# A streaming encoder layer on one core: other ticks for the heads' values, another start, a fixed order, and another order of the first convolution products

## The chip, the cores and the metric

The kernel runs on one core of one Trainium2 chip. Its time is the device time of one execution in microseconds (us). Three executions of the kernel before gave a median of 2348.04 us, the lowest 2346.84 and the highest 2348.41. One further execution was taken with the profiler; it took 2346.67 us, and its profile and trace are the ones read here. The engines are named as the profile names them: PE is the matrix engine, PEld its loads of the stationary operand, DVE the vector engine, ACT the scalar engine, POOL the third elementwise engine, and SP the engine whose queue issues most transfers (DMAs).

## What is computed

One layer of a hybrid encoder for 512 prompt frames and 64 frames of a running stream, 2048 channels wide, all in float32. Cut to what matters:

```python
hn = rmsnorm(x, g_norm1)
q, k, v, gb, gc, hc = split(hn @ w_in)            # 8 heads of 128, then 3 x 1024 for the convolution
q, k = rmsnorm(q, g_q), rmsnorm(k, g_k)           # per head
z = q @ k.T / sqrt(128)                           # strictly causal, 128-query blocks, cached keys first
log_1mb = where(mask, log_sigmoid(-z), 0)
after = reverse_cumsum(log_1mb) - log_1mb
o_attn = where(mask, exp(log_sigmoid(z) + after), 0) @ v      # stick-breaking weights
u = gc * hc
o_conv = gb * (conv_w[0]*u[t-2] + conv_w[1]*u[t-1] + conv_w[2]*u[t])
x = x + concat(rmsnorm(o_attn), rmsnorm(o_conv)) @ w_out
h2 = rmsnorm(x, g_norm2)
x = x + (silu(h2 @ w_gate) * (h2 @ w_up)) @ w_down
```

It returns the new frames, the new keys and values and the state of the convolution.

## The kernel before

**Numbers and tiles.** The 512 + 64 frames lie as 576 columns, cut into two halves of 288. A float32 product is made of three: each operand is split into a rounded high part and a remainder (`hi`/`lo`, `whi`/`wlo`, `ph`/`pl`, `vh`/`vl`), and high by high, low by high and high by low are added up in one accumulator. The high part is a cast, mostly on ACT (`cast`, line 727); the low part is a subtraction on DVE (`low`, line 730), which reads the cast. So each operand of PE costs one ACT and one DVE instruction, in this order.

**Stages.** In the order of time: *frames* (to about 33 us): x is loaded, turned by PE (`turn_samples`, line 384, for the 64 stream frames of a group of channels; `turn_x`, line 390, for the 512 others), copied by ACT into a tile `st` (lines 397, 399), and split by DVE into the two parts of `x` (lines 406, 407), while PE already multiplies by the first weight. *Projections* (to about 161 us): first whole products with `whi`/`wlo`, then, from about 72 us on, products that are cut into seven by sums of quarters (`unit_prepare` and `unit_run`; a product p_ of unit n is written (n, p_)). The sums of frames that these need are made by `x_sums` (lines 662 to 697, with DVE instructions on lines 677, 678, 680 and 681), one pair of channel groups after another. *Heads* (about 161 to 404 us): PE does the remaining projections (`pj`, line 246), and between their matmuls the work of the attention heads. *Convolution* (up to about 800 us, its own seven products per unit, `conv_prepare` and `conv_run`), mixed with the first parts of what follows; then the output projection and the feed-forward part.

**What sets the order.** Each engine runs its own queue in program order and waits at the head of it. The heads are generators: `attend(h)` yields at ticks. A tick is one step of a projection on PE, three matmuls of 288 columns. Head h starts PERIOD = 49 ticks after head h-1, so at any time the later ticks of one head lie between the early ticks of the next: tick 79 of a head and tick 30 of the next are the same moment. What a head does at its tick t is queued when PE's program has come to that tick. `until(t)` (line 745) waits for tick t.

In one head, `E` are the turned queries and keys, `sums` their squares' sums on DVE (line 777), `ss` the product that adds them up (line 784), `z` the scores, `ph`/`pl` the two parts of the log-weights `pb` of a query block, `zb` the sums over keys (lines 887 to 906), `limit` the step from these sums to the weights (DVE line 880, ACT line 882, cast), `vtok` the values, loaded back by `load_values`, `po` the product of weights and values (lines 931 and 934), `sp` and `cz` (lines 946 to 949) the sums for the 64 stream frames ("the sample"), and `os` their output.

Parts of the program run under a *manual schedule*: there the named engines keep the order in which the program is written; elsewhere the compiler's own scheduler may move instructions of an engine past each other. Before, the frames stage has a manual schedule for ACT, DVE and SP, the projections up to the units one for SP alone, and the units and heads one for ACT, DVE and POOL as well (`unit_mode`, line 1162).

In the convolution `corder` lists the products in PE's order, and `begin` says after which of them the next is prepared. `conv_prepare` makes the operand by sums on DVE (lines 1341 to 1359), a cast on ACT (1352) and a subtraction on DVE (1355). A column of raw weights is free, and the next one is loaded on SP (line 1318), when the last product that needs it has been prepared. `load_sum(q)` loads one of the three stored sums of frames, `xs_t`, of 2304 KB.

Of the kernel before, what the change touches and what calls it, by code (L numbers as in the profile page):

```python
# [98 lines left out]
def tile_hybrid_stream_step(  # L99
# [287 lines left out]
    def turn_x(kt, c, k, sc, pss):  # L387
        psx = ps_z.tile([P, 512], F32, tag=f"z{kt % 3}", name=f"psx{kt}")
        for i in range(4):
            nc.tensor.transpose(psx[:, i * P : (i + 1) * P], xin[c][:, i, k * P : (k + 1) * P], ident)  # L390
        if kt < NH:
# [11 lines left out]
        if kt >= 9 and kt % 2:  # L403
# [20 lines left out]
    with tc.manual_schedule(engines={mybir.EngineType.Activation, mybir.EngineType.DVE, mybir.EngineType.SP}):  # L424
# [26 lines left out]
        for kt in range(KD + LAG):  # L451
# [7 lines left out]
            for sc, (k0, k1) in enumerate(SCH):  # L459
                if kt == k0:  # L460
                    pss, psc = turn_samples(sc), sc
            if kt == 0:
                psg = misc("ps_g1")
                nc.tensor.transpose(psg[:, :KD], g1raw, ident[:KD, :KD])
                nc.vector.tensor_copy(out=g1c, in_=psg[:, :KD])
            for c, (k0, k1) in enumerate(XCH):
                if k0 <= kt < k1:
# [274 lines left out]
    def attend(h):  # L742
# [24 lines left out]
        yield until(9)  # L767
        for i, n in enumerate("qk"):
            if i:
                yield until(11)  # L770
# [4 lines left out]
        yield until(13)  # L775
# [6 lines left out]
        yield until(20)  # L782
# [7 lines left out]
        yield until(23)  # L790
# [3 lines left out]
        for i, n in enumerate("qk"):  # L794
            r = ms[:, NB * i : NB * (i + 1)].unsqueeze(2).to_broadcast([P, NB, 32])
            nc.vector.tensor_tensor(out=chunks(E[n]), in0=chunks(E[n]), in1=r, op=ALU.mult)
            yield until(25 + 2 * i)
# [3 lines left out]
        yield until(28)  # L801
        nc.scalar.activation(out=qf, in_=qf, func=AF.Copy, scale=gqs)
        cast(qh, qf[:, :TP])
        yield until(30)
        nc.scalar.activation(out=kf, in_=kf, func=AF.Copy, scale=col("gk"))
        cast(kh, kf[:, : 3 * P])
        yield until(31)
        low(ql, qf[:, :TP], qh)
        yield until(33)
        low(kl, kf[:, : 3 * P], kh)  # L810
        yield until(35)
# [3 lines left out]
        yield until(46)  # L815
# [22 lines left out]
        yield until(48)  # L838
        scores(1)
        soft_log(pr[1], z[1][:, :384])  # L840
        yield until(49)
# [3 lines left out]
        yield until(51)  # L845
# [5 lines left out]
        yield until(53)  # L851
# [6 lines left out]
        yield until(54)  # L858
# [3 lines left out]
        yield until(56)  # L862
        low(pl[1], pb[1], ph[1])
# [4 lines left out]
        yield until(58)  # L868
        low(s1l, pb[2], s1h)
        cast(s0h, pb[1])  # L870
        yield until(60)
        cast(ph[0], pb[0])
        low(s0l, pb[1], s0h)
        load_values(h)
        yield until(62)
# [10 lines left out]
        yield until(70)  # L886
        mm(zb[3], trif, pb[3], stop=False, **kw)
        mm(zb[2][:, P:], neg1f, pb[3], stop=False, **kw)
        mm(zb[2], trir, ph[2], stop=False, **kw)
        mm(zb[2], trir, pl[2], stop=True, **kw)  # L890
        limit(2)
        yield until(73)
        mm(zb[1], trir, ph[1], stop=False, **kw)
        mm(zb[1], trir, pl[1], stop=False, **kw)
        mm(zb[1][:, P:], neg1r, s1h, stop=False, **kw)
        mm(zb[1][:, P:], neg1r, s1l, stop=True, **kw)
        limit(1)
        yield until(74)
        low(pl[2], pb[2], ph[2])
        cV = t1.tile([P, 4, P], F32, tag="cV", name="cV")  # L900
        nc.sync.dma_start(out=cV, in_=cv[:, h, :].rearrange("(i p) d -> p i d", p=P))
        yield until(76)
        mm(zb[0], trir, ph[0], stop=False, **kw)
        mm(zb[0], trir, pl[0], stop=False, **kw)
        mm(zb[0][:, P:], neg1r, s0h, stop=False, **kw)
        mm(zb[0][:, P:], neg1r, s0l, stop=True, **kw)
        limit(0)
        yield until(77)
        low(pl[1], pb[1], ph[1])
# [3 lines left out]
        yield until(79)  # L913
        low(vl, vtok[:, 0:3, :], vh)
        low(pl[0], pb[0], ph[0])
        nc.sync.dma_start(out=vp[:, h, :].rearrange("(i p) d -> p i d", p=P), in_=vtok[:, 0:4, :])
        nc.sync.dma_start(out=vs[:, h, :], in_=vtok[TS:, 4, :])
        yield until(80)
        sp = scratch[:, 1280 : 1280 + T]
        soft_log(sp[:, :320], zc)  # L920
        yield until(83)
# [7 lines left out]
        yield until(88)  # L929
# [5 lines left out]
        yield until(89)  # L935
# [1309 lines left out]
```

## Time and profile before

| | |
|---|---|
| median of three executions | 2348.04 us (2346.84 to 2348.41) |
| profiled execution | 2346.67 us |
| its span, first to last instruction | 2345.0 us |
| PE busy, share of the span | 2322.5 us, 99% |
| PEld busy | 2311.2 us, 99% |
| DVE, ACT, POOL busy | 1903.2, 1162.6, 281.8 us |
| clock granted to PE | 1.00 |

The profile lists, for each engine, the time in which it was busy and what ended its idle times. PE's instructions overlap, and the ends of matmuls are modelled, so PE's idle time is a lower bound of what a wait costs; the idle time of PEld at the same wait is mostly longer by 0.2 us and is the upper bound used here. A row of the timeline gives the start and the duration in us, the engine, the line, the operation, what is written and read, and in brackets how long the engine was idle before it and what it waited for.

### The profile page before, as it was taken

The page shows a single profiled execution, that of the slowest core. Times are in us where ns is not written, and L with a number is a line of the kernel's source. Part 1 is how long each engine was busy: PE and PEld are TensorE (multiplying, and loading weights), DVE is VectorE, ACT ScalarE, POOL GpSimd, SP SyncE. Part 2 cuts the span into 40 slices and gives each one's busy share as a digit, 9 for nine tenths or more (in the row PEclk, how much of TensorE's full clock was granted, in tenths as well). Part 3 has the DMA queues.
Part 4 walks back from the last instruction along what each step waited for, and adds up shares of the span by engine and source line. Part 5 has one row for each costly group of instructions (what it writes and reads, how often), then busy time and mean ns, then how long its engine had stood idle before and what let it go on. Part 6 is the DMA issues. An engine that isn't in the chain of part 4 may idle for free.

```text
span 2345.0 us, 43719 instructions
## 1 busy us (share of the span) xinstructions
PE 2322.5 (99%) x17461; PEld 2311.2 (99%) x17461; DVE 1903.2 (81%) x2841; ACT 1162.6 (50%) x2010; POOL 281.8 (12%) x392
## 2 busy tenths in 40 slices
PE   8999999999999999999999999999999999999999
PEld 8999999999999999999999999999999999999999
DVE  8976776788877889888888888888888777987886
ACT  7536677444445555444444444444444444444444
POOL 2002333121111220000000000000000001431121
PEclk9999999999999999999999999999999999999999
DMA  8775554874378555345354344344444936885643
GB/s 276 206 226 144 134 142 110 269 234 127 112 242 229 173 171 174 119 153 158 109 158 157 115 155 151 124 154 141 136 154 133 354 123 203 226 239 190 200 129 106
DMA packets 584644, 401.95 MB, mean 171 GB/s; under 512 B 91838, under 2 KB 571832, under 8 KB 584440
## 3 DMA queue, kind: packets, MB, share of 16 engines
q1 hardware_dynamic: 573512, 378.01, 51.7%
q0 software_dynamic: 10064, 20.65, 3.9%
q8 instruction: 137, 2.24, 0.4%
q10 hardware_dynamic: 864, 0.49, 0.1%
q14 instruction: 67, 0.55, 0.1%
HBM read 303.23 MB, written 95.86 MB: 170 GB/s over the span
## 4 chain that ended last, share of the span: by engine, by line
PE 89%; DVE 5%; ACT 2%; DMA 2%; issue 1%; POOL 0%; SPq 0%; ACTq 0%; DVEq 0%; POOLq 0%
PE psy L1895 35%; PE psw L1895 18%; PE psx L1895 9%; PE psy L1383 6%; PE pj L246 6%; PE pjo L246 4%; PE psw L1383 3%; PE psy L1032 2%; PE psx L1383 1%; PE psw L1032 1%; DVE wlo L208 1%; DMA raw_a<-in_w_in_dram 1%; PE psx L1032 1%; PE po L934 0%; PE z L833 0%
## 5 line engine op out<-in xcount | busy, mean ns | idle before, releaser
L1895 PE MATMUL psy<-h_s,whl 128*128 128x288 f32 x2787 | 411.3, 294 | 0.0
L1895 PEld LDWEIGHTS psy<-h_s,whl 128*128 128x128 f32 x2787 | 383.4, 188 | 0.0
L256 DVE TENSOR_TENSOR whl<-raw_a,whl 128x1024 fp32r<-128x1024 f32 (+4 forms) x296 | 318.2, 1076 | 55.5 <-ACT whl L255 54.6
L1895 PE MATMUL psw<-t,whl 128*128 128x288 f32 x2400 | 347.7, 295 | 0.0
L1895 PEld LDWEIGHTS psw<-t,whl 128*128 128x128 f32 x2400 | 327.3, 188 | 0.3 <-DVE whl L256 0.2
L255 ACT CAST whl<-raw_a 128x1024 fp32r<-128x1024 f32 (+4 forms) x296 | 268.1, 907 | 103.0 <-issue 35.4
L246 PE MATMUL pj<-x,whi 128*128 128x288 f32 x1376 | 296.3, 299 | 1.4 <-DVE x L407 1.2
L256 DVE TENSOR_TENSOR whl<-raw_b,whl 128x1024 fp32r<-128x1024 f32 (+5 forms) x190 | 198.2, 1043 | 68.0 <-ACT whl L255 66.8
L255 ACT CAST whl<-raw_b 128x1024 fp32r<-128x1024 f32 (+5 forms) x190 | 165.5, 872 | 168.1 <-issue 73.0
L1905 ACT COPY part<-psy 128x288 f32<-128x288 f32 x242 | 96.5, 399 | 284.6 <-PE psy L1895 283.3
L246 PEld LDWEIGHTS pj<-x,whi 128*128 128x128 f32 x1376 | 227.3, 189 | 3.4 <-DVE x L407 2.4
L246 PE MATMUL pj<-x,wlo 128*128 128x288 f32 x688 | 203.3, 296 | 0.1
L1895 PE MATMUL psy<-b22m,whl 128*128 128x288 f32 x1212 | 183.0, 295 | 0.0
L1895 PE MATMUL psy<-t2t,whl 128*128 128x288 f32 x1212 | 182.6, 294 | 0.0
L1895 PE MATMUL psx<-h_s,whl 128*128 128x288 f32 x1185 | 173.1, 294 | 0.0
L1895 PEld LDWEIGHTS psy<-t2t,whl 128*128 128x128 f32 x1212 | 168.1, 189 | 0.2 <-DVE whl L256 0.2
L1895 PEld LDWEIGHTS psy<-b22m,whl 128*128 128x128 f32 x1212 | 167.9, 188 | 0.0
L1895 PEld LDWEIGHTS psx<-h_s,whl 128*128 128x128 f32 x1185 | 162.5, 188 | 0.0
L246 PEld LDWEIGHTS pj<-x,wlo 128*128 128x128 f32 x688 | 129.5, 188 | 1.0 <-DVE wlo L474 0.3
L255 ACT CAST whl<-s 128x1024 fp32r<-128x1024 f32 (+5 forms) x81 | 72.2, 892 | 100.4 <-PE psw L1895 100.3
L1674 POOL DMA_DIRECT2D hid_dram<-form x3 | 2.3, 757 | 971.1 <-DVE form L256 971.1
L1895 PE MATMUL psy<-t,whl 128*128 128x288 f32 x576 | 106.7, 295 | 0.0
(535 smaller groups left out, 4484.9 us busy)
## 6 DMA issues: line engine op xcount, KB each, us to landing
hid_dram<-form SPq DMA_DIRECT2D x147, 288.0 KB, 2.3
raw_a<-in_w_in_dram SPq DMA_DIRECT2D x33, 1024.0 KB, 5.4
raw_a<-in_w_gate_dram SPq DMA_DIRECT2D x22, 1024.0 KB, 5.7
raw_a<-in_w_up_dram SPq DMA_DIRECT2D x22, 1024.0 KB, 5.4
raw_b<-in_w_gate_dram SPq DMA_DIRECT2D x22, 1024.0 KB, 6.6
raw_b<-in_w_up_dram SPq DMA_DIRECT2D x22, 1024.0 KB, 7.5
h_s<-hid_dram SPq DMA_DIRECT2D x10, 2016.0 KB, 11.6
raw_a<-in_w_out_dram SPq DMA_DIRECT2D x16, 1024.0 KB, 5.7
```

Of the source, the lines that this page charges most:

```text
L208: nc.vector.tensor_tensor(out=lo[:, a : a + 1024], in0=raw[:, a : a + 1024], in1=hi[:, a : a + 1024].bitcast(F32), op=ALU.subtract)
L246: mm(ps, w_[:, k, csl], x_, start=(k == 0 and n == 0), stop=(k == nk - 1 and n == 2))
L255: nc.scalar.copy(out=hi, in_=src)
L256: (lo_eng or nc.vector).tensor_tensor(out=lo, in0=src, in1=hi.bitcast(F32), op=ALU.subtract)
L1032: mm(ps, whl[:, w_, j, :], x_, start=(start and j == 0 and q == 0), stop=(j == NP - 1 and q == 2), skip_group_check=True)
L1383: mm(ps, whl[:, w_, j, :], x_, start=(start and j == 0 and q == 0), stop=(j == m - 1 and q == 2), skip_group_check=True)
L1674: q.dma_start(out=hid_dram[fp][2 * n - 2 : 2 * n].rearrange("f p t -> p f t"), in_=t.bitcast(F32))
L1895: mm(ps, whl[:, w_, j, :], x_, start=(start and j == 0 and q == 0), stop=(j == len(xs_) - 1 and q == 2), skip_group_check=True)
L1905: nc.scalar.copy(out=t, in_=st["y"])
```

## The change

1. **Start.** At the first frames, the four turns of `x` (`psx0`) go ahead of the turn of the gains and of the stream frames; the small load of the gains `g1raw` moves from SP's queue to ACT's. The high part of channel group 3 is made by ACT and not by DVE.
2. **Fixed order.** `unit_mode` is opened some 40 lines further up, in front of the whole projections. `row_diagonals` becomes a generator that starts at tick 16 and is not written first any more.
3. **Heads.** Nearly all ticks of `attend` change. The squares' sums move from tick 13 to 12, and `ss`, which uses them, from 20 to 22. `load_values` moves from 60 to 56, the cast `vh` from 77 to 66 and `vl` from 79 to 67. The sample's `sp` is made at ticks 68 and 70 (from 80 and 83), its cast at 84 (from 89) and its low part at 86 (from 91). `zb`, `limit`, `po` and `cz` come two ticks later than they did.
4. **Convolution.** The products (0, 7) and (0, 6) stand ahead of (1, 2), and `load_sum(3)` is called after the third product and not ahead of the first. The tile `part7` of the convolution takes another buffer.

The same work is done; one instruction, the high part of group 3, becomes ACT's.

```diff
-        if kt >= 9 and kt % 2:
+        if kt == 3 or kt >= 9 and kt % 2:
             nc.scalar.activation(out=hi, in_=st, func=AF.Copy, scale=g1c[:, kt : kt + 1])
...
+        nc.scalar.dma_start(out=g1raw, in_=g_norm1[0].rearrange("(r c) -> r c", c=P))
         load_w0(0)
-        nc.sync.dma_start(out=g1raw, in_=g_norm1[0].rearrange("(r c) -> r c", c=P))
...
             if kt == 0:
+                def first():
+                    psg = misc("ps_g1")
+                    nc.tensor.transpose(psg[:, :KD], g1raw, ident[:KD, :KD])
+                    nc.vector.tensor_copy(out=g1c, in_=psg[:, :KD])
+                    heads_of["s"] = turn_samples(0)
+                    return heads_of["s"]
+                heads_of = {}
+                turn_x(0, 0, 0, 0, None, first)
...
-        yield until(13)
+        yield until(12)
         for i, n in enumerate("qk"):
             nc.vector.reduce_sum(out=sums[:, NB * i : NB * (i + 1)], in_=chunks(f[n]), axis=mybir.AxisListType.X)
...
-        yield until(20)
+        yield until(22)
         ss = misc("ss")[:, : 2 * NB]
         mm(ss, same, sums, start=True, stop=True)
...
         yield until(56)
+        load_values(h)
+        yield until(58)
...
+        yield until(66)
         vh = t1.tile([P, 3, P], F32R, tag="vh", name="vh")
         vl = t1.tile([P, 3, P], F32R, tag="vl", name="vl")
         cast(vh, vtok[:, 0:3, :])
-        yield until(79)
+        yield until(67)
         low(vl, vtok[:, 0:3, :], vh)
...
+        yield until(79)
+        low(pl[1], pb[1], ph[1])
+        yield until(81)
+        low(pl[0], pb[0], ph[0])
+        yield until(84)
+        sh = t1.tile([P, T], F32R, tag="sph", name="sph")
+        sl = t1.tile([P, T], F32R, tag="spl", name="spl")
+        cast(sh, sp)
+        yield until(86)
+        low(sl, sp, sh)
+        yield until(90)
         po = misc("po")
...
-    row_diagonals()
+    unit_mode = ExitStack()
+    unit_mode.enter_context(tc.manual_schedule(engines={mybir.EngineType.Activation, mybir.EngineType.DVE,
+                                                        mybir.EngineType.Pool}))
+    def diagonals():
+        row_diagonals()
+        yield from ()
+    pipe.spawn(diagonals(), 16)
...
-    load_sum(3)
     open_units()
-    corder = [(0, 1), (0, 2), (1, 1), (1, 2), (0, 7), (0, 6), (0, 5), (0, 3), (0, 4), (1, 6), (1, 7), (1, 5)]
+    corder = [(0, 1), (0, 2), (1, 1), (0, 7), (0, 6), (1, 2), (0, 5), (0, 3), (0, 4), (1, 6), (1, 7), (1, 5)]
...
+        if k_ == 2:
+            load_sum(3)
```

**Place 1: ACT at a head's values.** ACT's queue around the first head's cast of the values, before. `pr` and `z` belong to this head, `qf`, `qh`, `kf` and `kh` to the next one, `whi` to a projection's weight, and the three instructions on `raw_a` (lines 733 to 735) to this head's `sp`.

```order
L205 CAST whi_2483<-raw_a 128x1024 x2
L882 ACTIVATE pr_2305<-z_2302 128x384
L727 CAST ph_2308<-pr_2305 128x384
L882 ACTIVATE pr_2304<-z_2301 128x512
L727 CAST ph_2307<-pr_2304 128x512
L802 ACTIVATE qf<-qf,gqs 128x576
L727 CAST qh<-qf 128x512
L727 CAST vh<-vtok 128x384
L805 ACTIVATE kf<-kf,vec 128x576
L727 CAST kh<-kf 128x384
L733 ACTIVATE raw_a<-raw_a 128x320
L734 ACTIVATE raw_a<-raw_a 128x320
```

The same place now (line numbers are about ten higher):

```order
L737 CAST vh<-vtok 128x384
L743 ACTIVATE raw_a<-raw_a 128x320
L744 ACTIVATE raw_a<-raw_a 128x320
L745 ACTIVATE raw_a<-raw_a 128x320
L798 ACTIVATE raw_a<-raw_a 128x36
L799 ACTIVATE raw_a<-raw_a 128x36
L205 CAST whi_2490<-raw_a 128x1024 x2
L894 ACTIVATE pr_2316<-z_2313 128x384
L737 CAST ph_2319<-pr_2316 128x256
L894 ACTIVATE pr_2315<-z_2312 128x384
L737 CAST ph_2318<-pr_2315 128x384
L894 ACTIVATE pr_2314<-z_2311 128x512
```

The cast `vh` stood behind the last weights of the head and two instructions of the next head; now it stands in front of all three blocks' weights. The three instructions for `sp` went with it, and the two casts of the weight `whi` now precede the first block's weights.

**Place 2: DVE at the frames.** DVE's queue from the first split of x, before; `x` on lines 406 and 407 is the split, `xsq` and `xr` on lines 677 to 681 belong to `x_sums`.

```order
L406 TENSOR_SCALAR x_156<-st_225,g1c 128x2x288
L407 SCALAR_TENSOR_TENSOR x_156<-st_225,g1c,x_156 128x2x288
L182 TENSOR_TENSOR wlo_181<-raw_a,whi_180 128x512
L406 TENSOR_SCALAR x_156<-st_237,g1c 128x2x288
L677 SCALAR_TENSOR_TENSOR xsq_616<-st_225,g1c,xsq_616 128x288
L407 SCALAR_TENSOR_TENSOR x_156<-st_237,g1c,x_156 128x2x288
L406 TENSOR_SCALAR x_157<-st_247,g1c 128x2x288
L678 SCALAR_TENSOR_TENSOR xsq_618<-st_225,g1c,xr_617 128x288
L407 SCALAR_TENSOR_TENSOR x_157<-st_247,g1c,x_157 128x2x288
L406 TENSOR_SCALAR x_157<-st_257,g1c 128x2x288
L680 TENSOR_TENSOR xr_617<-xr_617,xsq_616 128x288
L407 SCALAR_TENSOR_TENSOR x_157<-st_257,g1c,x_157 128x2x288
```

Now:

```order
L408 TENSOR_SCALAR x_156<-st_225,g1c 128x2x288
L409 SCALAR_TENSOR_TENSOR x_156<-st_225,g1c,x_156 128x2x288
L182 TENSOR_TENSOR wlo_181<-raw_a,whi_180 128x512
L408 TENSOR_SCALAR x_156<-st_237,g1c 128x2x288
L409 SCALAR_TENSOR_TENSOR x_156<-st_237,g1c,x_156 128x2x288
L408 TENSOR_SCALAR x_157<-st_247,g1c 128x2x288
L409 SCALAR_TENSOR_TENSOR x_157<-st_247,g1c,x_157 128x2x288
L409 SCALAR_TENSOR_TENSOR x_157<-st_257,g1c,x_157 128x2x288
L408 TENSOR_SCALAR x_158<-st_278,g1c 128x2x288
```

The four instructions of the first pair's sums have left the splits (they stand behind all of them, after the row sums), and the high part of `st_257`, channel group 3, is no longer DVE's.

**Place 3: SP at the convolution's start.** SP's queue at the loads of `x`'s sums, of the sum `xs_t` and of raw weight columns, before:

```order
L1511 DMA x_161<-xs_dram 128x2x288
L1511 DMA x_162<-xs_dram 128x2x288
L1511 DMA x_163<-xs_dram 128x2x288
L1211 DMA xs_t_5808<-xs_dram 128x16x288
L1318 DMA raw_a<-in_w_in_dram 128x16x128 x2
L1318 DMA raw_c<-in_w_in_dram 128x16x128
```

Now:

```order
L1531 DMA x_161<-xs_dram 128x2x288
L1531 DMA x_162<-xs_dram 128x2x288
L1531 DMA x_163<-xs_dram 128x2x288
L1338 DMA raw_a<-in_w_in_dram 128x16x128
L1231 DMA xs_t_5905<-xs_dram 128x16x288
L1338 DMA raw_a<-in_w_in_dram 128x16x128
```

One column of raw weights goes ahead of the sum `xs_t`, which product (0, 4) reads.

More of the change, by code (lines that the diff above doesn't have):

```diff
@@ L385, in turn_samples, with turn_x @@
         return pss
-    def turn_x(kt, c, k, sc, pss):
+    def turn_x(kt, c, k, sc, pss, between=None):
         psx = ps_z.tile([P, 512], F32, tag=f"z{kt % 3}", name=f"psx{kt}")
@@ L390, in turn_x @@
             nc.tensor.transpose(psx[:, i * P : (i + 1) * P], xin[c][:, i, k * P : (k + 1) * P], ident)
+        if between:
+            pss = between()
         if kt < NH:
@@ L912, in attend @@
         cast(vh, vtok[:, 0:3, :])
-        yield until(79)
+        yield until(67)
         low(vl, vtok[:, 0:3, :], vh)
[L915 to L918, printed above, removed]
+        yield until(68)
         sp = scratch[:, 1280 : 1280 + T]
         soft_log(sp[:, :320], zc)
-        yield until(83)
+        yield until(70)
         soft_add(sp[:, :320], zc)
@@ L934, in attend @@
                 mm(po[:, i * P : 512], a_[:, i, :], b_[:, : 512 - i * P], stop=(i == 0 and n == 2), **kw)
-        yield until(89)
+        yield until(91)
         nc.scalar.copy(out=o_attn[h][:, :TP], in_=po)
-        sh = t1.tile([P, T], F32R, tag="sph", name="sph")
-        sl = t1.tile([P, T], F32R, tag="spl", name="spl")
-        cast(sh, sp)
-        yield until(91)
-        low(sl, sp, sh)
         ws = sp[:, :384]
         nc.gpsimd.memset(ws[:, :TS], 0.0)
-        yield until(98)
+        yield until(100)
         cz = misc("cz")
```

106 lines of the change are left out of this document (50 added, 56 removed).

## The prediction

> **What bounds the kernel now.** I read the page's busy times first, then the stages, then what PE waited for.
>
> ```profile
> PE 2322.5 (99%) x17461; PEld 2311.2 (99%) x17461; DVE 1903.2 (81%) x2841; ACT 1162.6 (50%) x2010; POOL 281.8 (12%) x392
> ```
>
> PE sets the time: 2345.0 - 2322.5 = 22.5 us without a matmul is all that a change of order can win, or 33.8 us by PEld. The second view cuts the span into stages (columns: length, then busy time and count of PE, PEld, DVE, ACT and POOL, clock, DMA share, GB/s).
>
> ```profile
> 0.00:33.00 33.00, 26.07 (x181) 23.73 (x182) 26.33 (x52) 22.93 (x67) 8.42 (x22) 1.00 0.83 253
> 33.00:77.00 44.00, 44.00 (x333) 43.81 (x333) 39.92 (x96) 32.88 (x86) 5.23 (x8) 1.00 0.76 260
> 161.00:404.00 243.00, 234.36 (x1706) 228.05 (x1706) 169.25 (x313) 165.03 (x322) 74.03 (x132) 1.00 0.52 140
> 520.00:1400.00 880.00, 880.00 (x6652) 879.40 (x6651) 738.07 (x1061) 426.53 (x692) 68.39 (x83) 1.00 0.50 156
> ```
>
> PE's idle time lies in the frames (33.00 - 26.07 = 6.9 us, most of it before the first data) and the heads (8.6 by PE, 15.0 by PEld); the wait for `whl` below adds 2.1 to 2.6 at the first convolution products. From 33 to 77 us PE has none, and 333 matmuls in 44.00 us give 0.132 us each: a tick of three is 0.40 us, a product of 24 is 3.17 us. After 520 us nothing is there to win. Third, the waits (total, times, longest), of PE and then of PEld:
>
> ```profile
> PE po L934 <- ACT vh L727: 4.3, 4, 1.8
> PE psy L1383 <- DVE whl L1355: 2.1, 2, 1.3
> PE ss L784 <- DVE raw_a L777: 1.8, 3, 1.1
> PE pj L246 <- DVE x L407: 1.2, 2, 1.0
> PE cz L947 <- DVE spl L730: 1.1, 3, 0.4
> PE po L934 <- DVE vl L730: 0.8, 4, 0.2
> PE cz L946 <- ACT sph L727: 0.4, 1, 0.4
> PEld po L934 <- ACT vh L727: 5.1, 4, 2.0
> PEld psy L1383 <- DVE whl L1355: 2.6, 2, 1.5
> PEld ss L784 <- DVE raw_a L777: 2.5, 3, 1.3
> PEld pj L246 <- DVE x L407: 2.4, 4, 1.3
> PEld cz L947 <- DVE spl L730: 1.8, 3, 0.6
> PEld po L934 <- DVE vl L730: 1.6, 4, 0.4
> PEld cz L946 <- ACT sph L727: 1.2, 3, 0.6
> ```
>
> Each of them is a wait that a part of the change addresses. The sum of PE's rows, 11.7 us, and of PEld's, 17.2 us, bound the whole gain.
>
> **The change part by part.** I make the sum against the profiled execution's 2346.67 us, which is 1.37 us below the median; the same difference is then taken from the median.
>
> *Frames.* Of PE's 1.2 us, 1.0 is one wait (start, duration, row):
>
> ```profile
> 13.35 1.77 POOL L182 TENSOR_TENSOR wlo<-raw_a,whi 128x512 fp32r<-128x512 f32 x1 [8.52 <-ACT whi L181]
> 13.90 1.83 DVE L407 SCALAR_TENSOR_TENSOR x<-st,g1c,x 128x576 fp32r<-128x576 f32 x1
> 15.79 0.54 PE L246 MATMUL pj<-x,whi 128*128 128x288 f32 x2 [1.04 <-DVE x L407]
> 16.09 0.51 DVE L681 SCALAR_TENSOR_TENSOR xr<-st,g1c,xr 128x288 f32<-128x288 f32 x1
> 16.52 0.81 DVE L407 SCALAR_TENSOR_TENSOR x<-st,g1c,x 128x576 fp32r<-128x576 f32 x1
> ```
>
> The split that took 1.83 us, against 0.81 for the same shape, lies beside POOL's instruction. Four instructions of `x_sums`, 0.51 us each (the row at 16.09), leave DVE's queue here, and one of 0.5 moves to ACT: 2.5 us of lead for the splits, more than the 1.3 us of the longest wait. That this wait vanishes gives 1.0 to 1.3 us, and the next ones up to PEld's 2.4. The turns that go first start earlier, but later frames still arrive when they arrive, so I give them nothing. I take 1.6 us, between 1.0 and 2.4. What left the queue stands in 33 to 77 us, where DVE has 44.00 - 39.92 = 4.1 us to spare: four times 0.51 fit, at no cost while that cover lasts.
>
> *The sums `ss`.* Two ticks later on PE, one earlier on DVE: 3 x 0.40 = 1.2 us against a longest wait of 1.1 (PE) or 1.3 (PEld). All but a remnant goes: 1.8 to 2.5, I take 1.9.
>
> *The sample's `cz`.* The cast is five ticks sooner and `cz` two later, 7 x 0.40 = 2.8 us against waits of at most 0.6. Gone: 1.5 (PE's two rows) to 3.0, I take 2.0.
>
> *The values and `po`.* This is the largest term and the least certain. Around the first head:
>
> ```profile
> 201.94 0.27 DVE L880 SCALAR_TENSOR_TENSOR z<-z,acA 128x128 f32<-128x128 f32 x1
> 202.12 0.54 DVE L730 TENSOR_TENSOR pl<-pr,ph 128x384 fp32r<-128x384 f32 x1
> 202.17 1.57 POOL L799 TENSOR_TENSOR Ek<-Ek,rpad_t 128x576 f32<-128x576 f32 x1 [7.82 <-DVE kf L798]
> 202.87 0.62 ACT L727 CAST ph<-pr 128x512 fp32r<-128x512 f32 x1
> 203.06 0.38 PE L931 MATMUL po<-pr,vtok 128*128 128x128 f32 x2
> 205.74 0.68 DVE L730 TENSOR_TENSOR pl<-pr,ph 128x512 fp32r<-128x512 f32 x1
> ```
>
> Ahead of `vh` ACT casts the next head's queries; eleven ticks sooner it is 4.4 us earlier, and no wait for `vh` or `vl` is left. What is late next is block 0. Its cast ends at 202.87 + 0.62 = 203.49, so its low part can be there at 203.49 + 0.68 = 204.17. `zb` and `po` both move by two ticks, so PE keeps its distance: it would begin at 203.06 and need that low part for the last of `po`'s eleven matmuls. The ten before it have 2 x 128, 3 x 256, 3 x 384 and 2 x 512 columns, 3200; at 0.132 us for 288 that is 1.5 us, so 204.5. That leaves 0.4 us. But two things eat it: the two `whi` casts now stand ahead of the blocks' weights on ACT, and DVE's subtraction for the weight waits for them with `limit` behind it, up to one cast of about 1 us; and POOL's product on line 799 can hold up a subtraction:
>
> ```profile
> 252.10 1.59 POOL L579 TENSOR_TENSOR acc_a<-acc_a,raw_a 128x288 f32<-128x288 f32 x2
> 252.31 1.94 DVE L730 TENSOR_TENSOR pl<-pr,ph 128x512 fp32r<-128x512 f32 x1
> ```
>
> Here it began 0.21 us after POOL and took 1.94 instead of 0.68 us, whereas at 202.12 it began 0.05 before POOL and took no longer. The Trainium skill, "SBUF — State Buffer", section "SBUF: two separate sides", says that a DVE instruction with two inputs in that memory and a POOL instruction that reads it exclude one another for a whole instruction, whoever starts first. Both rows agree: 252.10 + 1.59 = 253.69, and from there to 254.25 the subtraction has about its own time.
>
> So a head in which line 799 wins loses 1.3 us, about what it waited for `vh`; one in which it loses waits for almost nothing. The bounds are 0 (the wait changes its name) and 6.7 (PEld's 5.1 + 1.6). I take 3.7, a little over half.
>
> *Convolution.* The two waits begin with a load that lands late:
>
> ```profile
> 484.14 0.47 SPq L1211 DMA_DIRECT2D xs_t<-xs_dram  x1
> 490.45 5.85 SPq L1318 DMA_DIRECT2D raw_a<-in_w_in_dram  x2
> 499.41 1.23 DVE L1341 TENSOR_TENSOR raw_a<-raw_a,raw_c 128x1024 f32<-128x1024 f32 x1 [1.90 <-DMA raw_a<-in_w_in_dram]
> 499.60 3.33 PE L1383 MATMUL psw<-xs_t,whl 128*128 128x288 f32 x24
> ```
>
> The sum at 499.41 waited for a column of raw weights, and a cast and two more steps of DVE follow before PE has its operand. That column, 1024 KB, stood behind the 2304 KB of `xs_t`, while the transfers ran without a pause (480 to 505 us in 40 slices):
>
> ```profile
> GB/s 323 291 332 192 194 265 354 407 411 371 391 389 395 372 389 394 391 393 391 393 395 370 382 378 352 349 350 347 343 335 351 347 348 222 39 6 0 0 0 0
> ```
>
> Now it comes free one product sooner, at 490.45 - 3.17 = 487.3, and goes first. At about 370 GB/s 2.36 MB take 6.4 us: it lands some 6 us earlier, and the 2.1 to 2.6 us of the two waits go. The price is paid by `xs_t`. Both together were there at 499.4; in the other order the same bytes are there at the same time, and that is now the time of `xs_t`, which product (0, 4) reads at 499.60. This leaves 0.2 us, and nothing if the transfers pause because the first of the two is issued at 487.3 and not at 484.14 (at most the 3.2 us between). Also, the operand of (0, 7), one product sooner, is now made just in time. So from -0.6 to 2.6; I take 1.2.
>
> *Sum.* 1.6 + 1.9 + 2.0 + 3.7 + 1.2 = 10.4 us. From this I take 1.0 for waits that the new fixed order and the shifted ticks create somewhere (bounds 0 and the 2.0 us of one of DVE's waits in that stretch, below): 9.4 us. 2346.67 - 9.4 = 2337.3 for a profiled execution, and 2348.04 - 9.4 = 2338.6 for the median.
>
> **The rivals.**
>
> *A: `po` still waits, now for `pl`* (20%). The wait for `vh` turns into a wait of the same size for block 1's or 0's low part, since POOL's line 799 starts, as before, within 0.1 us of a subtraction. For it speaks the row at 252.31, against it the row at 202.12. The term 3.7 is gone: 2348.04 - 5.7 = 2342.3. By the rule of the Trainium skill named above, "SBUF — State Buffer", every head in which POOL starts first would go this way, by however little.
>
> *B: `xs_t` is late* (10%). For half of those 3.2 us the transfers pause: 1.6 us of waiting at (0, 4) in place of the 1.2 us won: 2338.6 + 1.2 + 1.6 - 2.1 = 2339.3 if the old waits go all the same, 2338.6 + 1.2 + 1.6 = 2341.4 if they do not. I give it the latter.
>
> *C: the values are not there at tick 66* (5%). They are loaded ten ticks, 4.0 us and a few other matmuls, ahead of the cast:
>
> ```profile
> DMA to landing us min/median/max: 3.2/5.1/6.9
> ```
>
> (the larger of the two loads, from the row's own line 969). At the worst 2.9 us are missing and ACT's queue stands with the next head's statistics and `whi` behind it. ACT is busy 165 of 243 us, so I expect the median's 1.1 us to be hidden; if half of 2.9 came through in each of four heads, 5.8 us, it is 2344.4.
>
> *D: slower through the fixed order* (5%). Between 33 and 77 us ACT, DVE and POOL now keep the order in which the program is written. DVE's own waits there (all there are):
>
> ```profile
> DVE dg L557 <- POOL rst L493: 2.0, 1, 2.0
> DVE xf L256 <- ACT xf L255: 1.8, 1, 1.8
> ```
>
> If each of the eight pairs of sums made DVE wait 1.8 us at its head, that is 14.4 us, of which 4.1 less the 2.0 us moved in are covered, and PE waits for the rest, 12.3 us: 2338.6 + 12.3 = 2350.9. It decides as soon as such waits exceed 9.4 + 2.1 = 11.5 us. Against it: no PE wait at all stands in this stretch now.
>
> *E: `po` is cured altogether* (13%): 6.7 in place of 3.7, 2335.6.
>
> **How the numbers follow.** The forecast has 47%, and its own range is 2336 to 2341. The range for 8 in 10 takes in E, A and B with the bounds of their terms: 2333.5 to 2345.0. Up to about 0.2%, 4.7 us, a measurement cannot tell this kernel from the one before: faster means below 2343.3. The forecast, B, E and most of A and a part of C lie there: 0.83. The rest of A and C and the milder forms of D are "the same", 0.13; D in full, 0.04.
>
> **What the changed profile would show.** Right: no PE wait for `vh` or `vl`, none for `raw_a` at `ss` over 0.3 us, none at `cz`; in the first 33 us no split of x that holds PE up by 1 us; in the heads' stage some 8 us more of PE's work in the same length; `po` waiting, where it waits, for `pl`. A head's wait for `pl` should go with a subtraction of more than 1 us beside line 809 (799 now) on POOL. At the convolution, `raw_a`'s first sum no longer waits for a DMA. Wrong: a PE wait between 33 and 161 us (D), a long ACT idle time at `vh` (C), PE waiting for `xs_t` at 495 to 500 us (B), or gaps of PE that no part of the change names.

## The result and the profile after

| | before | after |
|---|---|---|
| median of six executions | 2348.22 us (2346.84 to 2349.83) | 2334.69 us (2333.75 to 2334.94) |
| profiled execution | 2346.67 us | 2334.90 us |
| its span | 2345.0 us | 2333.2 us |
| PEld busy | 2311.2 us | 2311.3 us |

The ratio is 0.9941, with a 95% interval of 0.9929 to 0.9954: 13.5 us by the medians, 11.8 us between the two profiled executions. The one before happened to be a quick one for its kernel (2346.67, against a median of 2348.22). Five executions later in this study, the changed kernel had a median of 2333.97 us (2331.80 to 2335.07).

First, where PE stands at the same places of the program. These are rows of single lines on PE, with the start of the first and the last such matmul at the end; before:

```profile
L246 PE MATMUL pjz<-x,whi x32: 292/294/380, 39.1 to 45.5; 128*128 128x288 f32 x32
L1383 PE MATMUL psy<-x,whl x624: 291/294/398, 474.2 to 677.1; 128*128 128x288 f32 x156
L246 PE MATMUL pjo<-mixm,whi x480: 291/294/298, 766.8 to 867.8; 128*128 128x288 f32 x160
```

and after:

```profile
L246 PE MATMUL pjz<-x,whi x32: 292/294/377, 38.8 to 45.3; 128*128 128x288 f32 x32
L1403 PE MATMUL psy<-x,whl x624: 292/294/298, 463.5 to 664.8; 128*128 128x288 f32 x156
L246 PE MATMUL pjo<-mixm,whi x480: 292/294/297, 754.7 to 855.7; 128*128 128x288 f32 x160
```

At 39 us PE is 0.3 us ahead, at the first product of the convolution 10.7 us, at the output projection 12.1 us. So the frames gave 0.3, the heads (from 39 us on, with the projections ahead of them) 10.4 and the convolution 1.4 us; behind that 0.3 us are given back. The stages of the changed kernel (columns as in the prediction):

```profile
33.00:77.00 44.00, 44.00 (x334) 43.81 (x333) 42.97 (x102) 34.18 (x87) 5.85 (x9) 1.00 0.77 263
161.00:404.00 243.00, 242.09 (x1783) 237.52 (x1783) 180.04 (x327) 172.40 (x335) 73.78 (x137) 1.00 0.53 141
```

In the same 243 us of the heads, PE is now busy for 7.7 us more and starts 77 more matmuls. Between 33 and 77 us DVE is at 42.97 of 44.00 us, 3.1 more than before, and PE still has no gap. What PE and PEld wait for now (sum in us, times, the longest), apart from the program's first loads:

```profile
PE psw L1403 <- ACT whl L1372: 1.3, 1, 1.3
...
PE po L954 <- ACT ph L737: 0.4, 1, 0.4
PE po L954 <- DVE pl L740: 0.4, 1, 0.4
PEld po L954 <- DVE pl L740: 1.7, 3, 0.7
PEld po L954 <- ACT ph L737: 1.0, 2, 0.6
PEld ss L794 <- DVE raw_a L787: 0.2, 1, 0.2
```

No wait for `vh`, `vl`, `spl` or `sph` is left, and 0.2 us at `ss`. What stays at `po` is mainly in the first head (1.8 of the 2.7 us of PEld's two rows, the rest in the third):

```profile
193.36 0.51 ACT L737 CAST vh<-vtok 128x384 fp32r<-128x384 f32 x1 [1.20 <-DMA vtok<-vt_dram]
196.32 1.98 ACT L205 CAST whi<-raw_a 128x1024 fp32r<-128x1024 f32 x2
197.39 1.38 DVE L208 TENSOR_TENSOR wlo<-raw_a,whi 128x1024 fp32r<-128x1024 f32 x1 [0.97 <-ACT whi L205]
203.74 0.27 DVE L892 SCALAR_TENSOR_TENSOR z<-z,acA 128x128 f32<-128x128 f32 x1
203.91 0.54 DVE L740 TENSOR_TENSOR pl<-pr,ph 128x384 fp32r<-128x384 f32 x1
203.95 1.58 POOL L809 TENSOR_TENSOR Ek<-Ek,rpad_t 128x576 f32<-128x576 f32 x1 [6.26 <-DVE kf L808]
204.51 0.44 PE L954 MATMUL po<-pl,vh 128*128 128x384 f32 x1 [0.38 <-DVE pl L740]
```

Here ACT waits 1.20 us for the load of the values, and the two casts of `whi` stand ahead of the blocks' weights; DVE waits 0.97 us for them, and the last `limit` comes at 203.74 where it came at 201.94; 0.8 us of this are the two ticks by which the change itself moves it. The subtraction at 203.91 itself took its usual 0.54 us: POOL's product on line 809 began 0.04 us after it.

At the convolution the product (0, 4) waits now:

```profile
477.12 1.89 SPq L1231 DMA_DIRECT2D xs_t<-xs_dram  x1
479.81 1.06 ACT L1372 CAST whl<-raw_a 128x1024 fp32r<-128x1024 f32 x1
486.67 1.22 DVE L1361 TENSOR_TENSOR raw_a<-raw_a,raw_c 128x1024 f32<-128x1024 f32 x1
490.27 3.45 PE L1403 MATMUL psw<-xs_t,whl 128*128 128x288 f32 x24 [1.26 <-ACT whl L1372]
```

The sum on DVE no longer waits for its column. The profile names ACT's cast as PE's releaser, but the last cast on ACT ahead of that product began at 479.81 and took 1.06 us; what is late is the load of `xs_t`, issued at 477.12 (experiment 8). In the profiles of experiments 3, 4, 6, 7, 10 and 12 the same wait, 0.6 to 1.0 us of PE's idle time, is put down to this load by name.

### The profile page after: what moved, and what is told of

It is laid out like the page before. It is cut to its first block, busy times and chain, and to the rows that moved or that the text cites. A ratio compares the mean times of both kernels' runs of the same rounds, so it can differ in the third digit from the quotient of the medians.

```text
span 2333.2 us, 43719 instructions
## 1 busy us (share of the span) xinstructions
PE 2320.5 (99%) x17461; PEld 2311.3 (99%) x17461; DVE 1906.7 (82%) x2840; ACT 1163.6 (50%) x2011; POOL 273.2 (12%) x392
## 4 chain that ended last, share of the span: by engine, by line
PE 95%; DVE 2%; ACT 1%; DMA 1%; issue 0%; SPq 0%; POOL 0%; ACTq 0%; DVEq 0%; POOLq 0%
PE psy L1916 36%; PE psw L1916 18%; PE pj L246 9%; PE psx L1916 9%; PE psy L1403 7%; PE pjo L246 4%; PE psw L1403 4%; PE psy L1047 2%; PE psx L1403 2%; PE psw L1047 1%; PE psx L1047 1%; PE z L843 0%; DVE wlo L208 0%; PE po L954 0%; DMA Eq<-qk_dram 0%
```

## The experiments

All experiments were timed against the kernel before on the same chip, the first four, the next four and the last four each together, each four on another chip; the medians of the kernel before were 2348.79, 2348.80 and 2348.86 us there. The executions of one changed kernel span 2 to 5.5 us here (10.8 in experiment 5), and the 95% intervals of the ratios reach 2 to 3 us to either side. So a difference below about 3 us between two of these kernels isn't resolved by their medians, and the waits of the profiles are read beside them.

### 1. The heads' ticks alone

```diff
 (before, with attend() of the change and nothing else)
```

> The kernel before with the new ticks of the heads alone. Between the same places of the program the heads' stage got shorter by about 10.4 us in the changed kernel's trace. Theory 1 (the ticks alone did this): about 10.4 us below the kernel before, 2337.8 us. Rival (part of it is owed to the fixed order of the projections, which comes ahead of the heads): 7.6 us or less, the prediction's three terms, 2340.6 us or more.

2336.87 us against 2348.79 (ratio 0.9947, 0.9933 to 0.9961): 11.9 us. The waits of PEld between 161 and 520 us:

```profile
PEld psy L1388 <- DVE whl L1360: 2.6, 2, 1.5
PEld po L944 <- DVE pl L730: 1.6, 3, 0.6
PEld po L944 <- ACT ph L727: 1.1, 2, 0.7
PEld ss L784 <- DVE raw_a L777: 0.3, 1, 0.3
```

The heads look as in the changed kernel, and the convolution's 2.6 us are those of before. The ticks are nearly the whole change, and they don't need the fixed order.

### 2. The fixed order alone

```diff
-    row_diagonals()
+    unit_mode.enter_context(tc.manual_schedule(engines={...Activation, ...DVE, ...Pool}))
+    pipe.spawn(diagonals(), 16)
```

> The kernel before with the fixed order alone (and row_diagonals at tick 16). The first pair's sums leave the frames, the start is the old one. Theory 1 (the four DVE instructions caused the stall of the split at 15.8 us): this stall of 1.0 to 1.3 us is gone, PE comes to its full pace at 10.2 us as before, and the time is 1.0 to 1.6 us lower, 2346.9 us. Rival D of the prediction: DVE falls behind between 33 and 77 us and the time is above that of before. A second rival (the stall came from POOL's product beside the split and stays): no change.

2349.23 us against 2348.79 (ratio 0.9998, 0.9990 to 1.0007): no difference. The stall of 1.04 us at the split is gone from the profile, and PE has no wait between 33 and 161 us, so rival D doesn't occur. But in the profiled execution PE came to its full pace only at 14.5 us, though its start is the old one:

```profile
12.51 1.11 PE L390 MATMUL psx<-ident,xin 128*128 128x128 f32 x4
14.72 0.60 PE L390 MATMUL psx<-ident,xin 128*128 128x128 f32 x4
```

Four turns of the same shape take 1.11 us at 12.51 and 0.60 at 14.72. The expected 1.0 to 1.6 us weren't measured; the interval would still hold them.

### 3. The old start in the changed kernel

```diff
-        nc.scalar.dma_start(out=g1raw, ...)
         load_w0(0)
+        nc.sync.dma_start(out=g1raw, ...)
...
-                turn_x(0, 0, 0, 0, None, first)
+                pss, psc = turn_samples(sc), sc      # stream frames, then the gains, then turn_x
```

> The changed kernel with the old start: stream frames and gains turned first, the gains loaded on SP. Theory P (PE runs at half its pace until it has been busy without a longer pause; the new start's wait of 0.70 us at 8.4 us keeps it slow until 13.2 us, where the old one was slow until 10.2 us): full pace from about 10.2 us on, and 1.3 to 1.6 us less than the changed kernel, 2333.2 us. Rival (the start is bound by the loads, and the new one is simply as early as these allow): within 0.4 us of the changed kernel.

2333.14 us (2330.97 to 2334.37), with full pace from 9.9 us on: in the profile about 2.0 us ahead of the changed kernel at 16 to 33 us. That is what theory P said, but the profiled execution was the quickest of its five, and the changed kernel's own five executions beside experiment 12 had 2333.97. So no gain of the new start is seen, and whether it costs 1 us isn't settled.

### 4. PE kept busy ahead of the first product

```diff
+        def warm(n):
+            for _ in range(n):
+                nc.tensor.transpose(q0ps[1][:, :P], ident, ident)
+        warm(12)
...
                 def first():
+                    warm(3)
...
+            if kt == 1:
+                warm(4)
```

> The changed kernel with 19 turns of the identity, which nobody reads, in PE's pauses before the first product (12 ahead of the first frames, 3 ahead of the gains, 4 ahead of the third channel group). Theory P: PE is at its full pace by 8 to 10 us and the time falls by 1.6 to 1.9 us, until the loads bind: 2332.9 us. Rival (half pace belongs to the first seconds of a load or to the data, not to pauses): full pace still from 13.2 us on and no gain, or a loss of up to 0.5 us through the added turns.

PE's pace changes as theory P says. In the changed kernel, then with the added turns:

```profile
8.38 1.97 PE L390 MATMUL psx<-ident,xin 128*128 128x128 f32 x8 [0.70 <-DMA xin<-in_x_prompt_dram]
```

```profile
8.33 1.09 PE L390 MATMUL psx<-ident,xin 128*128 128x128 f32 x8 [0.39 <-DMA xin<-in_x_prompt_dram]
```

The eight turns take 1.09 and not 1.97 us, and at 33 us PE is 1.6 us ahead of the changed kernel. The time didn't follow: 2335.63 us (2335.25 to 2340.41). In the profiled execution the gain is lost again far behind: PEld waits 1.0 us at 690 us for `whl`, and 1.6 us at 2280 us for ACT's copy of a sum (experiment 8). So the pace is shown, a gain in time isn't.

### 5. The values late again

```diff
         yield until(56)
-        load_values(h)
...
         low(s0l, pb[1], s0h)
+        load_values(h)
...
-        yield until(66)
-        cast(vh, vtok[:, 0:3, :])
-        yield until(67)
-        low(vl, vtok[:, 0:3, :], vh)
...
         low(pl[1], pb[1], ph[1])
+        cast(vh, vtok[:, 0:3, :])
         yield until(81)
+        low(vl, vtok[:, 0:3, :], vh)
         low(pl[0], pb[0], ph[0])
```

> The changed kernel with the heads' values late again: loaded at tick 62, cast at 79 and low part at 81, as far ahead of the product po as before. Theory 1: the waits for vh and vl return in half of the heads, 3.7 us (the prediction's term) to 6.7 us: 2338.4 to 2341.4 us. Rival (po is bound by block 0's low part anyway, and only the name of the wait changed): within 1 us of the changed kernel.

2345.19 us (ratio to the kernel before 0.9986): 10.5 us above the changed kernel, and only 3.6 below the kernel before. PEld's waits between 161 and 430 us:

```profile
PEld po L951 <- ACT vh L737: 6.4, 5, 2.2
PEld po L951 <- DVE vl L740: 2.6, 7, 0.4
PEld ss L794 <- DVE raw_a L787: 0.4, 1, 0.4
```

9.4 us, where the changed kernel has 2.9 and the kernel before 12.2. The rival (`po` is bound by block 0 anyway) is out, and the time lies above the range of theory 1 too. By the waits, the values are worth 6.5 us at this place. By where PE stands they are worth more:

```profile
L246 PE MATMUL pjz<-x,whi x32: 292/294/379, 37.7 to 44.2; 128*128 128x288 f32 x32
L1400 PE MATMUL psy<-x,whl x624: 292/294/298, 471.7 to 671.9; 128*128 128x288 f32 x156
```

From the first of these products to the other the heads take 434.0 us here and 424.7 in the changed kernel, 9.3 us more. Added up in the trace from the start of each matmul to the start of the next, 8.2 of them lie at `po`, where the listed waits grew by 6.3: the idle time that the profile lists doesn't hold the whole cost of a wait. What the median has beyond 9.3 us is less than the executions of this kernel differ by (2342.56 to 2353.38).

### 6. The sums `ss` late again

```diff
-        yield until(12)
+        yield until(13)
...
-        yield until(22)
+        yield until(20)
```

> The changed kernel with the sums ss at tick 20 and their operand at 13 again. Theory 1: PE waits for the sums in three of eight heads, 1.8 to 2.5 us: 2336.5 to 2337.2 us. Rival (the sums are early enough in the new order of DVE): no change, 2334.7 us.

2334.49 us: no difference that can be measured. In the profile the wait is back, in two heads:

```profile
PEld ss L794 <- DVE raw_a L787: 1.8, 2, 1.4
PEld po L954 <- DVE pl L740: 0.7, 2, 0.5
PEld po L954 <- ACT ph L737: 0.4, 1, 0.4
```

and the waits at `po` are 1.6 us smaller than in the changed kernel. The sum of the three is the changed kernel's 2.9 us. That one wait has paid for the other (PE that stands at `ss` comes later to `po`) fits this, but it isn't shown: with the heads of the change untouched, the waits at `po` are between 1.3 us (experiment 3) and 2.7 us from one profile to another.

### 7. The sample's cast late again

```diff
-        yield until(84)
-        cast(sh, sp)
-        yield until(86)
-        low(sl, sp, sh)
...
         nc.scalar.copy(out=o_attn[h][:, :TP], in_=po)
+        cast(sh, sp)
+        yield until(93)
+        low(sl, sp, sh)
```

> The changed kernel with the sample's cast and low part behind po again (ticks 91 and 93), cz at 100. Theory 1: PE's waits at cz return, 1.5 to 3.0 us: 2336.2 to 2337.7 us. Rival (they only waited since the rest of the queue was late): no change.

2333.66 us, and no wait at `cz` in the profile at all; the theory fell. Cast and low part are as near to `cz` here as before (9 and 7 ticks). What remained of the change is that `sp` itself is made at ticks 68 and 70 and that the values are out of the way, so it was what comes ahead of the cast that was late, and not the tick of the cast. The values alone aren't it, since moving them alone makes the waits at `cz` longer (experiment 9); the earlier `sp` is the nearest candidate left, and no run moves it alone.

### 8. The last sum of frames in two halves

```diff
+        for j in range(0, NP, NP // parts):
+            nc.sync.dma_start(out=t[:, j : j + NP // parts].bitcast(F32),
+                              in_=xs_dram[q, j : j + NP // parts].rearrange("j f p t -> p j f t"))
```

> The changed kernel with the last stored sum of frames loaded in two halves. Theory X (PE's wait of 1.26 us at product (0, 4) is for that load, which lands 13 us after its issue): the first half is there in time, the second 1.6 us later than the first is needed: the wait is gone and the time falls by 1.0 to 1.3 us, 2333.5 us. Rival (the profile's name is right and the wait is for ACT's cast, or two loads land no earlier than one): no change.

The wait at product (0, 4) is gone; its row has no idle time before it:

```profile
489.28 3.33 PE L1405 MATMUL psw<-xs_t,whl 128*128 128x288 f32 x24
```

So it was for the load, as theory X has it, and not for ACT's cast, which is as before. The time is 2335.67 us (2333.40 to 2337.99), not lower. In the profiled execution PE waits 1.87 us for the third channel group at 9.4 us and 1.8 us at 2266 us:

```profile
2256.93 1.76 SPq L1804 DMA_DIRECT2D raw_a<-in_w_down_dram  x1
2265.23 0.72 ACT L255 CAST whl<-raw_a 128x640 fp32r<-128x640 f32 x1 [5.83 <-DMA raw_a<-in_w_down_dram]
2266.31 0.67 PE L1918 MATMUL psy<-t,whl 128*128 128x288 f32 x3 [1.77 <-ACT part L1928]
```

A weight lands late; ACT waits at the head of its queue for it, and the copy that PE needs stands behind. In the twelve profiles of this part the wait of PEld for that copy is between nothing and 3.5 us, the last in experiment 11. None of the edits touches this place.

### 9. The values alone

```diff
         yield until(54)
+        load_values(h)
...
+        yield until(64)
+        cast(vh, vtok[:, 0:3, :])
+        yield until(65)
+        low(vl, vtok[:, 0:3, :], vh)
         yield until(70)
 (on the kernel before; the old load, cast and low part are taken out)
```

> The kernel before with the values' load, cast and low part alone moved, by as many ticks ahead of po as in the change (load 54, cast 64, low part 65); the sums, the sample, the start, the order and the convolution stay. Theory V (the values are worth nearly all, since ACT and DVE give the time that the waits at po took back to what comes behind them): 8 to 10.5 us below the kernel before, 2339 to 2340.5 us, and the waits at cz shrink too. Rival (the ticks are worth something only together, as their prices in the prediction, 1.9 + 2.0 + 3.7): 3.7 to 6.7 us below, 2342 to 2345 us.

2343.99 us against 2348.86 (ratio 0.9979, 0.9970 to 0.9988): 4.9 us. Theory V fell, the rival's range holds. PEld's waits between 161 and 430 us:

```profile
PEld cz L949 <- DVE spl L730: 3.7, 7, 0.6
PEld ss L784 <- DVE raw_a L777: 3.2, 3, 1.4
PEld cz L948 <- ACT sph L727: 2.1, 4, 0.7
```

There is no wait at `po`. But the waits at `cz` have gone from 3.0 to 5.8 us and those at `ss` from 2.5 to 3.2: of the 6.7 us at `po`, 3.5 have moved on. PE's positions say the same of the heads alone:

```profile
L246 PE MATMUL pjz<-x,whi x32: 292/294/377, 38.8 to 45.2; 128*128 128x288 f32 x32
L1385 PE MATMUL psy<-x,whl x624: 292/294/398, 470.2 to 672.1; 128*128 128x288 f32 x156
```

From the one to the other PE takes 431.4 us here and 435.1 before, 3.7 us less. Taken alone, the values are worth 4.9 us by the medians and 3.7 by the heads' length; taken last (experiment 5), 10.5 and 9.3. The two differences of medians have intervals of some 2 and 3.5 us to either side, so the lengths are the better evidence; these too differ between executions, by 2.3 us for the heads before (437.4 us in experiment 2) and by 1.4 us for those of the change (423.4 to 424.8).

### 10. Block 1's low part behind POOL

```diff
         yield until(79)
+        nc.vector.memset(t1.tile([P, 64], F32, tag="late", name="late"), 0.0)
         low(pl[1], pb[1], ph[1])
```

> The changed kernel with one DVE instruction of about 0.1 us (a memset of 64 columns that nobody reads) ahead of the low part of block 1 in each head, so that this subtraction starts behind POOL's product of line 809 and not within 0.05 us of it. Rival A's mechanism: the subtraction then takes 1.8 to 2.0 us instead of 0.54, and where block 1's or 0's low part is the last that po needs, PE waits: up to 1.3 us in each of seven heads, 2337 to 2343 us. Other theory (po has room for it since the values come early): the subtraction is as slow, PE waits in the first head only, and the time is that of the changed kernel plus the 0.8 us of eight memsets at most.

A head of the changed kernel (in experiment 12's execution), DVE and POOL:

```profile
316.90 1.64 POOL L809 TENSOR_TENSOR Ek<-Ek,rpad_t 128x576 f32<-128x576 f32 x1 [1.43 <-DMA raw_a<-in_w_in_dram]
316.92 0.53 DVE L740 TENSOR_TENSOR pl<-pr,ph 128x384 fp32r<-128x384 f32 x1
```

and the same with the memset, POOL and DVE:

```profile
316.67 1.22 POOL L809 TENSOR_TENSOR Ek<-Ek,rpad_t 128x576 f32<-128x576 f32 x1 [1.43 <-DMA raw_a<-in_w_in_dram]
316.77 0.11 DVE L940 MEMSET late<- 128x64 f32 x1
316.81 2.10 DVE L740 TENSOR_TENSOR pl<-pr,ph 128x384 fp32r<-128x384 f32 x2
```

with the subtraction behind it, which the timeline merges with the next one, from the groups of instructions of that stretch (sum in us, mean in ns):

```profile
L740 DVE TENSOR_TENSOR pl<-pr,ph 128x384 fp32r<-128x384 f32 x1 | 1.5, 1496 | 0.0
```

Block 1's subtraction, 0.53 us long in the first fence, starts at 316.81, 0.14 us behind POOL, and takes 1.50 us, up to POOL's end at 317.89 and 0.4 beyond it. Now POOL takes 1.22 us, where it takes 1.64 when the subtraction comes first: whichever is first runs through, and the other pays. This bears out the rule of the Trainium skill, "SBUF — State Buffer", section "SBUF: two separate sides". It costs almost nothing here: the memset puts the subtraction behind POOL in four of the eight heads, the fourth to the seventh (1.50 or 1.51 us each), and only 0.2 us of wait at `po` lies in these. In all PEld waits 2.6 us there, the changed kernel 2.7 and, in experiment 12, 2.3. The time is 2336.29 us (2333.49 to 2336.62), between the two forecasts, and the medians can't tell it from the 2333.97 of experiment 12. By the waits, `po` has room for a late block 1, as the second theory has it. Rival A had the mechanism right and its cost wrong.

### 11. Old start, PE kept busy, load in halves

```diff
 (experiments 3, 4 (16 and 3 turns) and 8 together)
```

> The changed kernel with the old start, 19 turns of the identity in PE's pauses ahead of the first product, and the last stored sum loaded in two halves. If the start's slow pace and that load are what is left, full pace comes before 9 us, the wait at product (0, 4) is gone, and the time is 2 to 4 us below the changed kernel's on the same chip: 2331 to 2332.5 us. If the start is bound by the loads, and differences of 1 us in the profile are those between executions, it is within 1 us of the changed kernel.

PE is at its full pace from 5.2 us on at the latest (the four small turns at 5.15 us take 0.46 us; at half pace they take 0.69):

```profile
1.54 3.68 PE L456 MATMUL pj<-ident 128*128 128x128 f32 x16 [1.54 <-POOL ident masks.py:199]
5.15 0.46 PE L384 MATMUL psx_s<-ident,xsn 64*128 64x64 f32 x4
10.82 0.40 PE L384 MATMUL psx_s<-ident,xsn 64*128 64x64 f32 x3 [0.56 <-DMA xsn<-in_x_sample_dram]
```

It then waits for the loads (the second stream frames at 10.8 us), and the end of the program waits 3.5 us for the copies of experiment 8. The time is 2335.52 us (2334.39 to 2338.41). None of the three parts gives a time below the changed kernel's.

### 12. The changed kernel again

> The changed kernel itself once more, beside the three others on the same chip, so that differences of 1 to 2 us are read against it: 2333.8 to 2335 us as before.

2333.97 us (2331.80 to 2335.07); ratio to the kernel before on this chip 0.9938 (0.9926 to 0.9950). No other kernel of the study is faster by more than the executions differ. Its profile shows how much one execution differs from another: PE waits 0.5 us at `ss`, 0.4 at `po` and 0.7 for `xs_t`, where the first profile of this kernel has nothing, 0.8 and 1.3.

## Why the prediction was right, and where it was not

The direction and the wide range held: 2334.69 lies in 2333.5 to 2345.0. The forecast's own range, 2336 to 2341, did not: the gain was 13.5 us and not 9.4. The time is 0.9 us from the 2335.6 of rival E, but by luck, since E has `po` cured altogether, and 2.7 us of wait are left there. The sum itself came as near as it did because its errors had both signs: the frames were put 1.3 us too high, and against that `ss`, `cz`, `po` and the deduction for new waits were all too cautious. Step by step, by the profiled executions:

- **Frames** (1.6 us): 0.3. The stall at the split is gone, as the prediction has it. But the step "I give them nothing" for the new start failed: PE ran at half its pace until 13.3 us, 3.1 us longer than in the execution before, and that ate what the split gave. Experiments 2, 3 and 4 show that this is the pace of PE and differs between executions; with it the place at 39 us moves from 37.7 to 40.0 us in the seven profiles with the new start, so the 0.3 is one draw. The cover in 33 to 77 us held: DVE took 3.1 us more, PE waited for nothing.
- **`ss`** (1.9) **and `cz`** (2.0): 2.3 and 3.0 by PEld's rows, that is the upper ends of the ranges. I chose near PE's idle time; PEld's was the better price (from start to start of the matmuls, 2.4 and 3.3).
- **`po`** (3.7): 6.7 - 2.7 = 4.0 us by the waits, 5.2 from start to start. The term was near, though not for its reason. I kept nearly half of it back for POOL's product, which holds up no subtraction that `po` waits for (the 0.54 us at 203.91, experiment 10); in the second head it does hold one up, 1.29 us from 230.63 us on, and nothing waits. (The POOL row at 252.10 in the prediction is two products, 0.82 and 0.83 us, and the subtraction waited for both.) What does remain stands behind the other half of that step, the casts of `whi` ahead of the weights, and the late load of rival C, for which ACT waited 1.2 us in the first head and 1.1 in the fourth. No run takes either away; in the fourth head nothing at `po` waited, so the load alone isn't the cause.
- **Convolution** (1.2): 1.4. The old waits went, and 1.26 us of rival B came, at the named product (0.6 to 1.0 in six other profiles).
- **New waits** (-1.0): none between 33 and 161 us. Of this deduction only the upper bound had a row behind it, a wait of DVE and not of PE.

The terms so corrected sum to 0.3 + 2.3 + 3.0 + 4.0 + 1.4 = 11.0 us of the 11.8. The rest lies in the heads, 10.4 by the positions (10.5 unrounded) against 9.3 by the waits, and the trace says where: added up from the start of each matmul to the start of the next, which leaves nothing out, `po` gave 5.2 us, `cz` 3.3 and `ss` 2.4, and 0.3 were lost between them. So the idle time of PEld, called the upper bound of a wait ahead of the prediction, isn't one. Of the 1.7 us between 11.8 and the medians' 13.5, 1.5 are what the profiled execution before was faster than its median, and 0.2 what the one after was slower.

The step that failed most is one that isn't a term: that the three waits of the heads can be priced one by one. Experiments 5 and 9 show they can't. The same move of the values shortens the heads by 3.7 us alone and by 9.3 us as the last of the moves (4.9 and 10.5 by the medians). The waits of experiment 9 account for the first: from start to start, `po` gives 7.4 us, and 3.7 are lost again at `cz` and `ss`. That PE, not held at `po`, comes to these two earlier than their operands is the reason that fits; no run tests it apart from the rest. Why the waits at `po` are longer in experiment 5 than before the change (9.0 against 6.7 us of PEld's idle time) stays open.

## What to carry to other kernels

Waits of one engine that follow one another in a loop are better taken as one budget than as a list of prices: here, removing the largest alone moved half of it (3.5 of 6.7 us) to the next places. So move all of them ahead together, and judge each by leaving it out as well as by putting it in. Price a wait of PE by PEld's idle time rather than by PE's, and expect it to cost still more. Where two queues share work, look at what stands ahead of the late instruction (here the next head's queries ahead of `vh`, the making of `sp` ahead of its cast); for the sample's cast its own tick made no difference.

## What was not expected of the hardware

PE starts at half its pace, and the granted clock in the rows is 1.00 all the same: eight turns of 128 columns take 1.97 us and then 1.09 or less. The moment of the change differs between executions of the same start: 10.2 us (before), 12.6 (experiment 1), 14.5 (2), 9.9 (3) with the old one, 13.3 (after), 15.1 (8) and 11.4 (12) with the new one. With PE kept busy from 1.54 us on it came at 7.1 us (4) and by 5.2 us (11). The Trainium skill, "TensorE: Matmul & The Clock Gate", section "Part 1: The HAM clock gate (the "warmup" mystery)", says that the array is throttled to half until it has been busy for a window of about 3.4 us that runs freely. That fits the factor here, 213 against 109 ns from the start of one turn to the next. For the moment the same section of the Trainium skill gives a scatter of 500 ns under sustained work; with the pauses of these starts it lay anywhere in 5 us. That it is such a window, no run here shows.

The other is how sharp the exclusion of DVE and POOL is: a subtraction recorded 0.02 us behind POOL's start runs in 0.53 us, one 0.09 us behind (the first head of experiment 10) in 0.49, one 0.14 us behind takes 1.5 us, and an instruction of 0.11 us on DVE decides which.
